# The four slots of the split-weight ring made 32 bytes longer each

## The chip, the cores and the metric

The kernel runs on one core of a Trainium2 chip. The metric is device time in microseconds (us), the median of three runs. Engines are named as in the profile: PE is TensorE's matmul, PEld its weight load, DVE VectorE, ACT ScalarE, POOL GpSimd, SP SyncE, whose queue carries the loads.

## The reference

Two layers of a decoder trunk on 256 tokens of width 1024, in float32. Each layer is a mixer (sliding-window attention, gated short convolution and block attention, all fed by one input projection, each projected back and merged by sigmoid gates, then one output projection), a residual with LayerNorm, and a SwiGLU feed-forward of hidden width 2816 with another residual and LayerNorm:

```python
for l in range(DEPTH):
    mix = hybrid_mixer(x, w_in[l], attn_sinks[l], conv_w[l], w_branch_a[l],
                       w_branch_b[l], w_branch_c[l], w_out[l])
    x = layer_norm(ALPHA * x + mix, ln1_g[l], ln1_b[l])
    ffn = swiglu(x, w_ffn_gate[l], w_ffn_up[l], w_ffn_down[l])
    x = layer_norm(ALPHA * x + ffn, ln2_g[l], ln2_b[l])
```

Nearly all of the arithmetic is products of activations with weights that come once from HBM.

## The kernel before

**Split products.** A float32 product is made of three matmuls in the type float32r: a weight w is split into `wh` (ACT's copy, which rounds, L182) and `wl` = w - `wh` (DVE, L183), an activation likewise into a high and a low part, and wh·high, wh·low and wl·high are added up in PSUM.

**Weight pieces.** All weights lie in HBM as 142 pieces of 128 partitions x 2048 float32 (8192 bytes in each partition). SP loads each into one of three `raw` slots (`load`, from L141); ACT and DVE split it in two halves of 1024 columns (`parts`, L180 to L183) into a tile `wh` and a tile `wl`. Both tags have a ring of `RING = 4` slots in the pool `wts`, so there are eight such tiles. Six pieces of the 142 do not go through the ring: they are split into `wA` and `wB`, in the pool `keep` (the table `place`, L127 to L131).

**What PE does with them.** `mm(acc, a, b)` (L253) issues one matmul: `a` is the stationary operand, loaded by an LDWEIGHTS of 128 columns, and `b` the moving operand, which streams through. The kinds of matmul, by the name of the PSUM tile that they write:

| tile | made by | stationary | moving | columns | matmuls |
|---|---|---|---|---|---|
| acc | `whole` (L357) | wh, then wl | xx | 512, then 256 | 1152 pairs |
| gc | `merge`, `trio` | wh, wh, wl | xx | 256 | 384 |
| br | `branch`, `trio` | wh, wh, wl | y | 256 | 576 |
| hp | `half_pair`, `tokens` | xx | wh, wl, wh | 256 | 576, and 96 with wB |
| cv | `tokens` | xx | wh, wl, wh | 512 | 96 |
| pr, first projection of a layer | `project`, `tokens` | mx | wh, wl, wh | 512 | 144, and 48 with wA |
| pr, second, hidden 0 to 11 | `project` | hidA | wh, wl, wh | 512; 256 | 252; 72 |
| pr, second, hidden 12 to 21 | `project` | hidB | wh, wl, wh | 512; 256 | 168; 48, and 54 with wB |

The rest are 180 transposes (`tp`) and the attention's own products (`s`, `yp`). Of the 1152 pairs of acc, 576 belong to the two feed-forward stages, which run without other matmuls between (272 to 370 and 697 to 795 us of the span); the other 576 belong to the mixers, where `s`, `tp` and `yp` come between.

**What sets the order.** The order on each engine is written out by the class `Plan`, from fixed costs by columns; sizes of tiles do not enter it. The tiles' addresses come from the pools, in the order const, raws, wts, keep, work, each tile rounded up to 32 bytes. In the program as built every ring slot begins at 32 mod 128: `wh` at bytes 44960, 53152, 61344 and 69536 of a partition, `wl` at 77728, 85920, 94112 and 102304. `raw`, `xx`, `mx` and `hidB` begin at 32 mod 128 too; `y`, `hidA`, `wA` and `wB` at 64 mod 128. Each operand of a matmul begins a multiple of 512 bytes behind its tile's start, so it has its tile's residue.

**The start.** Piece 0 is loaded and split in five steps along the inner dimension (L305 to L313: steps of 1, 1, 2, 2 and 2 blocks of 128), each with two ACT copies (L274) and two DVE subtractions (L275), for `xx` and for `wh`, `wl`. PE multiplies each step as it comes.

Of the kernel before, what the change touches and what calls it, by code (L numbers as in the profile page):

```python
# [10 lines left out]
FR = mybir.dt.float32r  # L11
# [5 lines left out]
P = 128  # L17
# [7 lines left out]
PIECE = 2048  # L25
# [22 lines left out]


class Plan:  # L50
    """Orders the instructions of each engine by an estimate (us) of when they can start."""

    HOP = 0.09

# [59 lines left out]
def trunk(ctx: ExitStack, tc: tile.TileContext, x, xt, w, sinks, conv, ln, out):  # L114
# [4 lines left out]
    wts = pool("wts", RING)  # L119
    keep = pool("keep", 1)  # L120
    work = pool("work", 2)
# [1 line left out]
    ctx.enter_context(tc.manual_schedule(engines={ENG.PE, ENG.DVE, ENG.Activation, ENG.SP}))  # L123
    T = Plan()

    # Weight pieces: loaded and split ahead of their use, in the order in which they are used.
    place = {}  # L127
    for l in range(L):
        place[l * PER_LAYER + N_IN + N_BR + N_OUT - 1] = "A"
# [4 lines left out]
    spare, ready, chunks, raw, landed, rawfree = {}, {}, {}, {}, {}, {}  # L134
# [6 lines left out]
    def load(ks=None):  # L141
        j = pos["load"]
        if j >= total:
            return
        pos["load"] += 1
        raw[j] = raws.tile([P, PIECE], FT, name="raw")
        if ks is None:
            for s in cut(j):
                nc.sync.dma_start(raw[j][:, s], w[j][:, s])
        else:  # L150
            a, b = by_k(raw[j]), by_k(w[j])
            for k in ks:
                nc.sync.dma_start(xs[:, k, :], xt[:, k, :])  # L153
                nc.sync.dma_start(a[:, :, k, :], b[:, :, k, :])  # L154
        landed[j] = max(landed.get(j - 1, 2.5), rawfree.get(j - RAWS, 0.0) + 2.0) + 3.0
        open_splits()
# [4 lines left out]
    def open_splits():  # L161
        while pos["split"] < pos["load"]:
            j = pos["split"]
            if j in place:
                if place[j] not in spare:
                    return
                t = spare.pop(place[j])
                both = keep.tile([P, 2, PIECE], FR, tag=place[j], name="w" + place[j])
                ready[j] = both[:, 0, :], both[:, 1, :]
            else:  # L170
                if not slots:
                    return
                t = slots.pop(0)
                ready[j] = wts.tile([P, PIECE], FR, name="wh"), wts.tile([P, PIECE], FR, name="wl")
            pos["split"] += 1
            if j:
                split_piece(j, max(t, landed[j]))
# [7 lines left out]
    def split_piece(j, t, n=CHUNK):  # L185
        def last(task):
            rawfree[j] = task.ready
            load()

        need = T.pe + 5.2 * (j - pos["take"])  # L190
        ss = [slice(c, c + n) for c in range(0, PIECE, n)]
        chunks[j] = [T.add(parts(j, s), t - (1.5 if len(cut(j)) > 1 and not i else 0.0), max(need - t, 0.0) + 0.001 * i, last if s.stop == PIECE else None)
                     for i, s in enumerate(ss)]

    def take():
        j = pos["take"]
        pos["take"] += 1
        T.run()
        T.finish(*chunks.pop(j))
        return j  # L200

    def drop(j):
        if j in place:
            if j % PER_LAYER == N_IN + N_BR + N_OUT:
                spare["B"] = T.pe
        else:
            slots.append(T.pe)
        del ready[j]
        open_splits()

    # Tensor-engine work that waits for a result, issued once the engine has got that far.
    waiting, rounds = [], []
    busy = [0]

# [27 lines left out]
    banks = {"mm": [], "o": []}  # L242

    def bank(shape, tag, name):
        """The next PSUM bank; its last reader four tiles ago is waited for."""
        t = ps.tile(shape, FT, tag=tag, name=name)
        if len(banks[tag]) >= 4:
            for task in banks[tag].pop(0):
                T.finish(task)
        banks[tag].append([])  # L250
        return t, banks[tag][-1]
# [14 lines left out]
    def turn(src, n):  # L266
        tp, users = bank([P, n, P], "o", "tp")
        for i in range(n):
            nc.tensor.transpose(tp[:, i, :], src(i), ident)  # L269
            T.pe += pe_time(2 * P)  # L270
        return tp, users
# [11 lines left out]
    rings = {}  # L283

    def scratch(tag, bufs=2, shape=(P, S)):
        """A work tile for the next task; the task that had its slot before is that task's to wait for."""
        ring = rings.setdefault(tag, [])
        had = ring.pop(0) if len(ring) >= bufs else None
        ring.append(None)
        claims.append((ring, len(ring) - 1, had))  # L290
        return work.tile(list(shape), FT, tag=tag, name=tag, bufs=bufs)
# [60 lines left out]
    def gather(dst, acc):  # L352
        low = scratch("low", 3)
        return copy(low, acc[:, 1, :], S) + [
            dve(S) + (lambda: nc.vector.tensor_add(dst, acc[:, 0, :], low),)]  # L355

    def whole(done, by_step=False):  # L357
        j = take()
        wh, wl = duo(j)
        accs = [bank([P, 2, S], "mm", "acc") for m in range(2)]  # L360
        order = [(m, k) for m in range(2) for k in range(KD)]
        if by_step:
            order.sort(key=lambda mk: mk[1])
        for m, k in order:
            acc, users = accs[m]
            mm(acc, wh[:, m, k, :], xk[k], k == 0, False)
            mm(acc[:, 1, :], wl[:, m, k, :], xk[k][:, 0, :], False, k == KD - 1)
            if k == KD - 1:
                if m:
                    drop(j)  # L370
                done(m, acc, users)
                tick()

    def half_pair(js, h, last):
        acc, users = bank([P, 2, 2, P], "mm", "hp")
        for n in range(2):
            if len(js) == n:
                js.append(take())
            wv = duo(js[n])
            for k in range(KD):  # L380
                tokens(acc[:, n, :, :], [t[:, :, k, :] for t in wv], k, h, xk, k == 0, k == KD - 1)
            if last:
                drop(js[n])
            tick()
        return acc, users

    class Round:
        """A pair of heads: keys and queries split, head a's high part on its own 64 partitions."""

        def __init__(self, when, q, k, new_k, xq, xk, scores):  # L390
            self.when, self.q, self.k, self.new_k, self.xq, self.xk = when, q, k, new_k, xq, xk
# [236 lines left out]
    for l in range(L):  # L628
# [42 lines left out]
        for n in range(2):  # L671
            j = take()
# [16 lines left out]
        for j in range(2):  # L689
# [4 lines left out]
            def conv_h(m, acc, users):  # L694
                hh[m] = scratch("hh")
                made[m] = after(users, gather(hh[m], acc))

            def conv_c(m, acc, users):
                i = 2 * j + m
                t = scratch("t1")  # L700
                u = up[:, i, 2:]
                made[2 + m] = after(users, gather(t, acc) + [("G", 0.69, lambda: nc.gpsimd.tensor_mul(u, t, hh[m]))],
                                    needs=[made[m]])
                z = zs[m] = scratch("t2")

                tap = [cw[:, l, 4 * n + i:4 * n + i + 1].to_broadcast([P, S]) for n in range(3)]
                other = hh[m]

                def taps():
                    nc.gpsimd.tensor_mul(z, up[:, i, 0:S], tap[0])  # L710
                    for n in (1, 2):
                        nc.gpsimd.tensor_mul(other, up[:, i, n:S + n], tap[n])
                        nc.gpsimd.tensor_add(z, z, other)

                made[4 + m] = after([], [("G", 4.0, taps)], needs=[made[2 + m]])
# [87 lines left out]
        merge()  # L803
        spare["A"] = spare["B"] = T.pe
        open_splits()

        hid, last_f = [], {f: [] for f in range(NF)}
# [46 lines left out]
        last = l == L - 1  # L854
# [79 lines left out]
```

## Time and profile before

| | us |
|---|---|
| median of 3 runs (lowest, highest) | 867.87 (866.75, 868.48) |
| span of the profiled execution, first to last instruction | 864.6 |
| median less span | 3.3 |
| PE busy | 852.0 |
| DVE, ACT, POOL busy | 633.3, 485.6, 71.1 |

The profile gives the profiled execution's span and no device time of its own, so sums are made in the span and the 3.3 us are added. A matmul's busy time in the profile reaches past the start of the next one, since matmuls are pipelined: what one costs is read from start to start, or from a stretch of equal ones divided by their number. The chain of work that ended last is listed as stretches with a line and a count, which gives just that. "Idle before" is time in which the engine waited, with what released it.

### The profile page before, as it was taken

What the parts mean: (1) busy time and instruction counts of PE and PEld (TensorE: products, weight loads), DVE (VectorE), ACT (ScalarE), POOL (GpSimd) and SP (SyncE); (2) the same over time, 40 slices, a digit from 0 to 9 for tenths busy, and PEclk for the clock granted to TensorE, in tenths of its full rate; (3) what the DMA queues carried; (4) which work ended last, traced back from release to release, by engine and by line L of the source; (5) the groups of instructions that cost most, each with busy time, mean ns of one, the idle gap of its engine ahead of it and who ended that gap; (6) DMA issues with size and microseconds to landing.
All of it is one profiled execution on the core that took longest, in us unless ns stands there. A gap on an engine that the chain in (4) does not pass through costs nothing.

```text
span 864.6 us, 13385 instructions
## 1 busy us (share of the span) xinstructions
PE 852.0 (99%) x5222; PEld 748.1 (87%) x5222; DVE 633.3 (73%) x1105; ACT 485.6 (56%) x897; POOL 71.1 (8%) x94
## 2 busy tenths in 40 slices
PE   7999999999999999999999999999999999999996
PEld 5978888999899888888898888889998988888885
DVE  5688998766876777755657899986679577777435
ACT  6657677745535666544346767776555265565320
POOL 2003620000100000000000065000000000000000
PEclk9999999999999999999999999999999999999999
DMA  8854444464754555556336343345557365555511
GB/s 295 290 187 155 141 152 146 166 223 163 276 197 159 186 191 195 191 188 227 124 105 242 140 169 124 139 154 196 195 195 249 142 238 177 175 189 196 194 49 49
DMA packets 24815, 155.02 MB, mean 179 GB/s; under 512 B 2704, under 2 KB 4528, under 8 KB 7344
## 3 DMA queue, kind: packets, MB, share of 16 engines
q1 hardware_dynamic: 23536, 149.96, 49.0%
q0 software_dynamic: 1216, 4.22, 1.5%
q8 instruction: 41, 0.67, 0.3%
q14 instruction: 22, 0.18, 0.1%
HBM read 153.11 MB, written 1.05 MB: 178 GB/s over the span
## 4 chain that ended last, share of the span: by engine, by line
PE 97%; DMA 1%; SPq 1%; DVE 1%; ACT 0%; POOLq 0%; issue 0%
PE acc L254 46%; PE pr L254 19%; PE hp L254 9%; PE br L254 8%; PE gc L254 5%; PE s L254 3%; PE cv L254 3%; PE tp L269 2%; PE yp L468 1%; DMA raw<-w 1%; PE yp L470 0%; SPq L154 0%; SPq L153 0%; DVE xtok L496 0%; DVE wl L183 0%; ACT wh L182 0%
## 5 line engine op out<-in xcount | busy, mean ns | idle before, releaser
L254 PE MATMUL acc<-xx,wh 128*128 128x512 f32 x1152 | 411.5, 400 | 5.2 <-ACT wh L274 4.9
L183 DVE TENSOR_TENSOR wl<-raw,wh 128x1024 fp32r<-128x1024 f32 x266 | 325.2, 1243 | 98.5 <-ACT wh L182 97.3
L182 ACT ACTIVATE wh<-raw 128x1024 fp32r<-128x1024 f32 x266 | 272.5, 1052 | 101.8 <-PE pr L254 48.1
L254 PE MATMUL acc<-xx,wl 128*128 128x256 f32 x1152 | 324.8, 282 | 0.2 <-DVE wl L183 0.2
L254 PEld LDWEIGHTS acc<-xx,wh 128*128 128x128 f32 x1152 | 217.6, 189 | 56.7 <-ACT wh L274 6.2
L254 PEld LDWEIGHTS acc<-xx,wl 128*128 128x128 f32 x1152 | 218.9, 190 | 1.5 <-DVE wl L275 0.9
L278 ACT ACTIVATE low<-acc 128x256 f32<-128x256 f32 x144 | 54.2, 380 | 69.7 <-PE acc L254 69.5
L254 PE MATMUL hp<-wh,xx 128*128 128x256 f32 x384 | 72.1, 285 | 0.0
L254 PE MATMUL br<-y,wh 128*128 128x256 f32 x384 | 67.9, 280 | 0.0
L254 PE MATMUL pr<-wh,hidA 128*128 128x512 f32 (+1 forms) x216 | 61.7, 370 | 0.0
L254 PEld LDWEIGHTS hp<-wh,xx 128*128 128x128 f32 x384 | 60.7, 191 | 0.1
L254 PEld LDWEIGHTS br<-y,wh 128*128 128x128 f32 x384 | 59.0, 188 | 0.1
L355 DVE TENSOR_TENSOR t<-acc,low 128x256 f32<-128x256 f32 x88 | 37.0, 420 | 29.9 <-ACT low L278 29.8
L254 PE MATMUL hp<-wl,xx 128*128 128x256 f32 x192 | 54.3, 283 | 0.0
L254 PE MATMUL br<-y,wl 128*128 128x256 f32 x192 | 53.8, 280 | 0.0
L254 PE MATMUL gc<-xx,wh 128*128 128x256 f32 x256 | 46.1, 283 | 0.0
L254 PEld LDWEIGHTS pr<-wh,hidA 128*128 128x128 f32 x216 | 39.0, 188 | 7.7
L254 PE MATMUL pr<-wh,hidB 128*128 128x512 f32 (+1 forms) x144 | 41.9, 367 | 0.0
L499 POOL TENSOR_TENSOR mv<-mv,half 128x1 f32<-128x1 f32 x8 | 7.7, 963 | 398.0 <-DVE mv L490 398.0
L254 PE MATMUL pr<-wl,hidA 128*128 128x512 f32 (+1 forms) x108 | 40.0, 370 | 0.0
L254 PEld LDWEIGHTS gc<-xx,wh 128*128 128x128 f32 x256 | 39.9, 192 | 0.0
L254 PEld LDWEIGHTS hp<-wl,xx 128*128 128x128 f32 x192 | 36.8, 192 | 0.0
(130 smaller groups left out, 1073.1 us busy)
## 6 DMA issues: line engine op xcount, KB each, us to landing
raw<-w SPq DMA_DIRECT2D x136, 1024.0 KB, 4.8
gb<-ln POOLq DMA_DIRECT2D x8, 512.0 KB, 6.1
raw<-w SPq DMA_DIRECT2D x6, 512.0 KB, 6.8
xtok<-x SPq DMA_DIRECT2D x2, 512.0 KB, 6.7
xs<-xt SPq DMA_DIRECT2D x3, 256.0 KB, 4.8
raw<-w SPq DMA_DIRECT2D x3, 256.0 KB, 5.4
out<-xtok SPq DMA_DIRECT2D x3, 256.0 KB, 2.1
xs<-xt SPq DMA_DIRECT2D x2, 128.0 KB, 2.7
```

The lines of the kernel that those rows point to most:

```text
L182: return [act(n) + (lambda: nc.scalar.activation(wh[:, s], raw[j][:, s], AF.Copy),), dve(n) + (lambda: nc.vector.tensor_sub(wl[:, s], raw[ ...
L183: dve(n) + (lambda: nc.vector.tensor_sub(wl[:, s], raw[j][:, s], wh[:, s].bitcast(FT)),)]
L254: nc.tensor.matmul(acc, a, b, start=start, stop=stop)
L269: nc.tensor.transpose(tp[:, i, :], src(i), ident)
L278: return [act(n) + (lambda: nc.scalar.activation(dst, src, AF.Copy),)]
L355: dve(S) + (lambda: nc.vector.tensor_add(dst, acc[:, 0, :], low),)]
L468: nc.tensor.matmul(yp[los[a], :], v[:, 0, vsel[a]], pts[a][:, 0:2, :], start=True, stop=False)
L499: nc.gpsimd.tensor_tensor(mv[:, 3:4], mv[:, 2:3], half, op=OP.pow)
```

## The change

The tiles of the two rings are allocated with 2056 columns and used as their first 2048. A slot takes 8224 bytes of a partition in place of 8192:

```diff
@@ -171,7 +171,7 @@
                 if not slots:
                     return
                 t = slots.pop(0)
-                ready[j] = wts.tile([P, PIECE], FR, name="wh"), wts.tile([P, PIECE], FR, name="wl")
+                ready[j] = [wts.tile([P, PIECE + 8], FR, tag=t_, name=t_)[:, :PIECE] for t_ in ("wh", "wl")]
             pos["split"] += 1
```

The rest of the diff takes out comments and docstrings and keeps the line numbers. In the program as built, the slots then begin at these residues:

| | slot 0 | slot 1 | slot 2 | slot 3 |
|---|---|---|---|---|
| wh, byte of a partition | 44960 | 53184 | 61408 | 69632 |
| wh, mod 128 | 32 | 64 | 96 | 0 |
| wl, byte of a partition | 77856 | 86080 | 94304 | 102528 |
| wl, mod 128 | 32 | 64 | 96 | 0 |

All tiles behind them move up by 8 x 32 = 256 bytes and keep their residue. The two rings do not turn in step: the pieces use, one after the other, the residues (wh, wl) = (32, 32), (0, 0), (96, 64), (64, 96).

No instruction moves on any engine. On ACT, in the five steps of piece 0, the copies of steps 3 and 4 into `wh` wait for DVE besides their DMA (the subtraction that reads the step before):

```order
 L274 ACTIVATE wh<-raw 128x2x256 [waits DMAHW5_49]
 L274 ACTIVATE xx<-xs 128x2x256 [waits DMAHW6_49]
-L274 ACTIVATE wh<-raw 128x2x256 [waits DMAHW7_49]
+L274 ACTIVATE wh<-raw 128x2x256 [waits DMAHW7_49,DVE_49]
 L274 ACTIVATE xx<-xs 128x2x256 [waits DMAHW0_49]
-L274 ACTIVATE wh<-raw 128x2x256 [waits DMAHW1_49]
+L274 ACTIVATE wh<-raw 128x2x256 [waits DMAHW1_49,DVE_49]
```

The two waits are for DVE's sixth and eighth subtraction, the ones into `wl` of steps 2 and 3; each is made by one wait instruction ahead of the copy.

## Rows read from the trace of the kernel before

**Rows 1.** The page's head and engines: busy us, share of the span, instructions.
```profile
span 864.6 us, 13385 instructions
PE 852.0 (99%) x5222; PEld 748.1 (87%) x5222; DVE 633.3 (73%) x1105; ACT 485.6 (56%) x897; POOL 71.1 (8%) x94
PEclk9999999999999999999999999999999999999999
```
**Rows 2.** The page's chain that ended last, shares by engine and line.
```profile
PE 97%; DMA 1%; SPq 1%; DVE 1%; ACT 0%; POOLq 0%; issue 0%
```
**Rows 3.** Who PE waited for: us in total, times, longest.
```profile
PE acc L254 <- ACT wh L274: 4.9, 1, 4.9
PE acc L254 <- DVE xx L275: 0.2, 1, 0.2
PE acc L254 <- DVE wl L183: 0.2, 1, 0.2
```
**Rows 4.** The chain in order of time: start us, us, what, matmuls.
```profile
21.03 8.64 PE hp L254 x72
...
91.55 8.33 PE acc L254 x48
99.88 0.66 PE tp L269 x6
100.53 2.82 PE acc L254 x16
...
164.44 33.92 PE br L254 x288
198.36 23.02 PE gc L254 x192
...
271.86 98.93 PE acc L254 x560
```
**Rows 5.** Timeline of PE, second projection with hidA: start us, us, instruction.
```profile
378.09 0.63 PE L254 MATMUL pr<-wh,hidA 128*128 128x512 f32 x2
...
379.49 0.40 PE L254 MATMUL pr<-wh,hidA 128*128 128x512 f32 x1
```
**Rows 6.** Timeline of PE, second projection with hidB.
```profile
407.85 0.39 PE L254 MATMUL pr<-wl,hidB 128*128 128x512 f32 x1
...
409.21 0.39 PE L254 MATMUL pr<-wl,hidB 128*128 128x512 f32 x1
```
**Rows 7.** Timeline of PE, first projection, from piece wA to a ring piece.
```profile
230.84 1.56 PE L254 MATMUL pr<-wA,mx 128*128 128x512 f32 x6
232.24 0.39 PE L254 MATMUL pr<-wh,mx 128*128 128x512 f32 x1
...
233.40 0.62 PE L254 MATMUL pr<-wh,mx 128*128 128x512 f32 x2
...
234.08 0.62 PE L254 MATMUL pr<-wh,mx 128*128 128x512 f32 x2
```
**Rows 8.** Lines L182 and L183: duration ns min/median/max, first and last start.
```profile
L182 ACT ACTIVATE wh<-raw x266: 1037/1051/1071, 13.0 to 830.8; 128x1024 fp32r<-128x1024 f32 x133
L182 ACT ACTIVATE wB<-raw x8: 1046/1051/1066, 223.9 to 828.9; 128x1024 fp32r<-128x1024 f32 x8
L183 DVE TENSOR_TENSOR wl<-raw,wh x266: 1209/1220/1761, 14.1 to 832.4; 128x1024 fp32r<-128x1024 f32 x133
L183 DVE TENSOR_TENSOR wB<-raw,wB x8: 1215/1218/1226, 225.4 to 830.1; 128x1024 fp32r<-128x1024 f32 x8
```
**Rows 9.** Timeline of the start: ACT, DVE and PE in steps 2 to 4.
```profile
8.42 0.69 DVE L275 TENSOR_TENSOR wl<-raw,wh 128x512 fp32r<-128x512 f32 x1
...
10.36 0.63 ACT L274 ACTIVATE wh<-raw 128x512 fp32r<-128x512 f32 x1 [0.55 <-DMA raw<-w]
...
11.02 0.69 DVE L275 TENSOR_TENSOR wl<-raw,wh 128x512 fp32r<-128x512 f32 x1 [0.49 <-ACT wh L274]
...
11.72 0.63 ACT L274 ACTIVATE wh<-raw 128x512 fp32r<-128x512 f32 x1
...
12.97 1.06 ACT L182 ACTIVATE wh<-raw 128x1024 fp32r<-128x1024 f32 x1 [0.62 <-DMA raw<-w]
...
13.35 0.40 PE L254 MATMUL acc<-xx,wh 128*128 128x512 f32 x1
...
13.58 0.28 PE L254 MATMUL acc<-xx,wl 128*128 128x256 f32 x1
```

## The prediction

> **What bounds the kernel now.** I read the page's engines first: PE is busy 852.0 of 864.6 us, and its clock stands in the top tenth, the 2.4 GHz level, in every slice [rows 1]. The chain that ended last agrees: 97% of it is PE [rows 2]. Then who PE waited for: 5.3 us in three waits, all at the start [rows 3]. So behind the start nothing that ACT, DVE or the loads do ends last, and the change can act in one way alone: if PE's own matmuls go faster or slower because their weights begin elsewhere. What a matmul costs I take from stretches of the chain, each divided by its count [rows 4], and, for 512 columns, from PE's timeline, start to start.
>
> Pure streaming at 2.4 GHz would be 106.7 ns for 256 columns and 213.3 for 512. No kind reaches that, and the surplus differs with the starts of the two operands:
>
> - Weights and partner both at 32 mod 64: hp 8.64/72 = 120.0 ns, gc 23.02/192 = 119.9 [rows 4]; 512 columns with hidB, six matmuls from 407.85 to 409.21, 226.7 ns [rows 6].
> - One at 32 and the other at 64: br 33.92/288 = 117.8 ns [rows 4]; 512 columns with hidA, six from 378.09 to 379.49, 233.3 ns [rows 5]. With wA moving and mx stationary it is 233.3 as well: six from 230.84 to 232.24 [rows 7].
> - After such a stretch the equal kind doesn't find its pace at once: from 232.24 to 233.40 five matmuls take 232.0 ns each, and only then, from 233.40 to 234.08, three take 226.7 [rows 7].
> - The pairs of acc have equal starts throughout and yet two paces: 2 x 8.33/48 = 347.1 ns in the mixer, and behind the next transposes 2 x 2.82/16 = 352.5; 2 x 98.93/560 = 353.3 through a whole feed-forward stage [rows 4]. So the starts are not all: the pace into which PE falls also hangs on what ran just before, and it can keep the worse one for 99 us.
>
> Only two residues occur before, 32 and 64 mod 128; the change brings 0 and 96 as well. I reckon with mod 64: 96 as 32 and 0 as 64. No row shows that; it is my choice, since it needs no pace that the trace lacks.
>
> **The change part by part.** Counted in the program as built, by each matmul's own weight slice:
>
> 1. 256 columns. 288 of hp and 192 of gc go from equal to different: 480 x (117.8 - 120.0) = -1.1 us. 272 of br become equal: 272 x 2.2 = +0.6. Together -0.5 us. The 120 of 256 columns in the last projection I set at nothing; at 2.2 ns they are worth 0.3 us at most.
> 2. 512 columns. 40 of cv, 80 with mx and 84 with hidB go from equal to different: 204 x 6.6 = +1.3 us. Of those with hidA 134 become equal. But half of all pieces have wh and wl of different kind (96 with 64), so that equal and different alternate after one or two matmuls, and five are needed to find the pace [rows 7]. So of the 134 half get 226.7 (67 x 6.6 = -0.4) and half 232 (67 x 1.3 = -0.1), and of the 204 that stay equal with mx, hidB and cv half rise from 226.7 to 232: 102 x 5.3 = +0.5. Together +1.3 us.
> 3. acc, nearly half of the chain. No row has a pair with different starts. The nearest are 512 and 256 columns apart, 233.3 + 117.8 = 351.1 ns, and I take that. It lies between the two paces of now. In the feed-forward 288 of 576 pairs change: 288 x (351.1 - 353.3) = -0.6 us. In the mixers 288 change; by the chain some 320 of the 576 run at 346.7 to 347.1 and the rest at about 353, so 160 x 4.4 = +0.7 and 128 x -2.2 = -0.3. Of the 288 feed-forward pairs that stay equal, each piece now comes behind one of another kind, as those of the mixer come behind other work, and may fall into the better pace; I take one in four: 72 x -6.6 = -0.5. Together -0.7 us. The bounds are wide. Every pair at the best pace of the rows: 832 pairs (576 of the feed-forward, 256 of the mixers) x -6.4 = -5.3 us. Above, no row has a steady pace over 353.3; if the better pace were lost everywhere, 320 x 6.4 = +2.0, and if every one of the 576 changed pairs lost a further 7 ns, the step from one kind to the other that 512 columns show, +4.0: together +6.0.
> 4. ACT's writes and DVE's reads and writes of the slots. Ring halves at 32 take 1051 and 1220 ns (median), halves of wB, at 64, take 1051 and 1218 [rows 8]. Nothing; and were a half some tens of ns slower, ACT and DVE have slack (56% and 73% busy, and PE waits for neither behind the start).
> 5. The two new waits. Step 3's copy starts at 10.36, held by its DMA; the subtraction it now waits for began at 8.42 and took 0.69, so it is done at 9.11. Step 4's copy starts at 11.72; its new wait ends with the subtraction that runs from 11.02 to 11.71 [rows 9]. It slips by the passing of the semaphore and the wait instruction, by my estimate under 0.1 us (DVE follows ACT's copy of 10.36 to 10.99 at 11.02, 0.03 us). Behind it on ACT stands the next piece's copy, which waits for its DMA until 12.97 anyway; DVE's subtraction of step 4 would slip with it and end near 13.2 in place of 13.1. PE first wants this step's wh at 13.35 and its wl at 13.58 [rows 9]. Cost nothing; without that cover, 0.1 us.
> 6. Loads, the other tiles and their order: the raw slots stay where they are, tiles behind move by 256 bytes and keep their residue. Nothing.
>
> Sum: -0.5 + 1.3 - 0.7 = +0.1 us on a span of 864.6. With the 3.3 us around it: 868.0.
>
> A word on a rule that speaks against any such effect. The Trainium skill (SBUF — State Buffer, Specifications) has SBUF read in lines of 16 bytes. All starts, before and after, are multiples of 32, so by it every slice covers the same lines and each term above is nothing: the span would stay at 864.6. The rows agree with it for ACT and DVE and disagree for PE, where 117.8 stands against 120.0 and 233.3 against 226.7 with no other difference of columns; I hold to the rows.
>
> **The rivals.**
>
> *The good paces need all slots alike (slower).* 226.7 and 347 were only seen in runs of equal starts. If any change of residue between neighbours breaks them, and the unlike kind's gain for 256 columns doesn't come (br has other operands than gc, so its 117.8 may belong to y and not to the difference), then cv, mx and hidB pay 408 x 6 = +2.4 us, the mixers' 320 pairs +2.0, br 576 x 2.2 = +1.3: +5.7, 873.6. It starts to decide when more than a third of that arrives without the gains of term 1. For it: the relocking in rows 7. Against: gc and hp show nothing to break.
>
> *The change shakes the feed-forward out of its worse pace (faster).* PE keeps 353.3 for two whole stages because nothing disturbs it; in the mixers, behind other work, it falls into 347 for 48 matmuls at a time. With residues turning every 5.7 us, all pieces may settle at the better pace or below: -5.3 from term 3, with term 1's -0.5 and half of term 2: about -5, 863. For it: acc is nearly half of the chain. Against: half of the pieces mix their kinds and have no row at all.
>
> *The starts don't matter to PE, or the old ones are simply replaced by equals (no change).* Then 867.9, within the forecast's own range.
>
> *The new residues 0 and 96 have paces of their own.* No row speaks for or against; it widens the range to both sides.
>
> **How the numbers follow.** No change 0.38, slower 0.27, faster 0.35. A measurement of this kernel can tell about 0.2%, 1.7 us, from no change; my sum lies well inside, but its terms are of that size and each pace of acc is a guess between the rows, so the sides together get more than half; the faster side more than the slower, since more of the work runs at a bad pace now than at a good one (832 pairs against 320). The no-change case alone ranges over 866.3 to 869.7. The range for 8 in 10 goes from the faster rival's 863 less 1 to the slower rival's 873.6: 862 to 873.5.
>
> **What would show it.** PE's timeline: start to start of gc and hp pieces, 120.0 or 117.8 by the piece's residue; of hidB near 233 and of hidA a mixture; the feed-forward stage's length, 98.9 us now. It is right if that stage stays within 98 to 100 and the other stretches move by under 1 us each; wrong if one residue gives a pace that no row of before has, such as pairs well under 347 or over 354, or if PE waits for ACT or DVE behind the first 15 us.

## The result and the profile after

The changed kernel takes 862.36 us (862.00 to 862.64, five runs), before 867.87: ratio 0.9933, 95% interval 0.9913 to 0.9953. It is 5.5 us faster, outside the range that I gave for no change and near the figure of the faster rival (863). The spans of the two profiled executions differ by 4.0 us (864.6 and 860.6); the medians stand 3.3 and 1.8 us above them. In every execution whose span was taken, device time less its own span is 1.7 to 1.9 us, so the 3.3 us that the forecast added hold some 1.5 us by which the profiled execution of before was faster than the median one. The rows below explain the 4.0.

PE of the changed kernel still does 96% of the chain, and waits 5.6 us, 5.3 before [rows 2, 3]. Who PE waited for (us in total, times, longest):

```profile
PE acc L254 <- ACT wh L274: 5.4, 3, 4.5
PE tp L269 <- DVE xtok L496: 0.2, 1, 0.2
```

So the time came out of PE's own matmuls. The chain in order of time (start us, us, what, matmuls), to be laid beside [rows 4]:

```profile
21.23 8.51 PE hp L254 x72
...
91.51 8.37 PE acc L254 x48
...
100.53 2.79 PE acc L254 x16
...
164.49 33.89 PE br L254 x288
198.37 22.72 PE gc L254 x192
...
271.83 97.33 PE acc L254 x560
369.16 57.00 PE pr L254 x246
...
694.54 97.28 PE acc L254 x560
```

The two feed-forward stages fall from 98.93 us to 97.33 and 97.28: 347.5 ns a pair in place of 353.3, together -3.25 us. gc falls by 0.3 us a layer, hp from 120.0 to 118.2 ns a matmul, which is -1.0 us over its 576. br stays (33.92 and 33.89); the mixers' acc, added up start to start over both traces, falls by 0.4 us. The second projection of layer 0 took 56.85 us for its 246 matmuls and takes 57.00.

Within a stage the pace turns with the pieces. Two neighbouring pieces on PE's timeline (start us, us, instruction), the first with wh and wl at 32 mod 128, the second with both at 0:

```profile
299.51 0.39 PE L254 MATMUL acc<-xx,wh 128*128 128x512 f32 x1
...
300.55 0.39 PE L254 MATMUL acc<-xx,wh 128*128 128x512 f32 x1
...
303.32 0.40 PE L254 MATMUL acc<-xx,wh 128*128 128x512 f32 x1
...
304.37 0.39 PE L254 MATMUL acc<-xx,wh 128*128 128x512 f32 x1
```

Three pairs from 299.51 to 300.55 are 346.7 ns each, three from 303.32 to 304.37 are 350. The first piece has the residues of before mod 128 and yet the better pace, which before was seen only in the mixers. Mod 256 it does not have them: the four longer slots of wh push the whole ring of wl up by 128 bytes, so wl begins at 32 mod 256, where before it began at 160 like wh and xx.

### The profile page after: what moved, and what is told of

Read it like the earlier page. It is cut to its first block, busy times and chain, and to the rows that moved or that the text cites. A ratio compares the mean times of both kernels' runs of the same rounds, so it can differ in the third digit from the quotient of the medians.

```text
span 860.6 us, 13387 instructions
## 1 busy us (share of the span) xinstructions
PE 847.7 (99%) x5222; PEld 746.6 (87%) x5222; DVE 633.9 (74%) x1105; ACT 486.8 (57%) x897; POOL 71.3 (8%) x94
## 4 chain that ended last, share of the span: by engine, by line
PE 96%; DMA 2%; DVE 1%; SPq 0%; issue 0%; ACT 0%; POOLq 0%; POOL 0%; DVEq 0%
PE acc L254 47%; PE pr L254 18%; PE hp L254 9%; PE br L254 8%; PE gc L254 5%; PE s L254 3%; PE cv L254 3%; PE tp L269 2%; PE yp L468 1%; DMA gb<-ln 1%; DMA raw<-w 1%; PE yp L470 0%; DVE xtok L496 0%; SPq L153 0%; DVE wA L183 0%
## 5 line engine op out<-in xcount | busy, mean ns | idle before, releaser
L183 DVE TENSOR_TENSOR wl<-raw,wh 128x1024 fp32r<-128x1024 f32 x266 | 325.4, 1244 | 97.2 <-ACT wh L182 96.0
L182 ACT ACTIVATE wh<-raw 128x1024 fp32r<-128x1024 f32 x266 | 273.0, 1054 | 101.1 <-PE pr L254 49.0
L254 PEld LDWEIGHTS br<-y,wl 128*128 128x128 f32 x192 | 36.2, 188 | 0.0
```

Of the source, the lines that this page charges most:

```text
L182: return [act(n) + (lambda: nc.scalar.activation(wh[:, s], raw[j][:, s], AF.Copy),), dve(n) + (lambda: nc.vector.tensor_sub(wl[:, s], raw[ ...
L183: dve(n) + (lambda: nc.vector.tensor_sub(wl[:, s], raw[j][:, s], wh[:, s].bitcast(FT)),)]
L254: nc.tensor.matmul(acc, a, b, start=start, stop=stop)
```

## The experiments

Distances are counted in bytes from xx (160 mod 256), or for br from y (192), to wh and wl, mod 256; before, all pieces are at (0, 0) from xx, and in the changed kernel none is. Theory A says that it takes residues which turn from piece to piece, B and C that each distance has a pace of its own (B counts mod 128, C mod 256), H that PE holds one of several steady paces at the same starts, chosen by what ran before.

**Uniform residues: u32, u64, u96, u0.** Slots of 8320 bytes, 65 x 128, used from column `o` = 0, 8, 16 or 24:

```diff
-                ready[j] = wts.tile([P, PIECE], FR, name="wh"), wts.tile([P, PIECE], FR, name="wl")
+                ready[j] = [wts.tile([P, PIECE + 32], FR, tag=t_, name=t_)[:, o:o + PIECE] for t_ in ("wh", "wl")]
```

Expected of u32: 

> All eight ring slots 8320 bytes long and used from their first byte, so that every weight begins at 32 mod 128 as before, but neighbours differ by 128 mod 256; the two added ACT waits are not there. Theory A (turning: the residues that alternate from piece to piece throw PE out of the 353.3 ns cycle; equal residues leave it in whatever cycle it entered): 867.9, feed-forward stage 98.9 us. Theory B (own pace: each distance between the two operands' starts has a pace of its own, whatever ran before): the changed kernel's pieces with 32 and 32 ran at 346.9 ns a pair, so 864 to 865 and a feed-forward stage of 97.1 us. If the length of the slot or 256 mattered, neither.

Expected of u64: 

> All weights of the ring at 64 mod 128, nothing turning. Theory A: no gain from turning; pairs of acc keep one pace through the stage, by the rows for unlike starts 350 to 351, feed-forward 98.0 to 98.3 us, whole kernel 866 to 868. Theory B: the pair's pace depends on the distance of weights from xx (32 bytes here); the changed kernel's pieces at 0 (distance -32) ran at 350, so again 350 and 98.0; br (y at 64, distance 0) 120.0, gc and hp 117.8: 866 to 867. Theories differ little here; what counts is whether 64 and 0 cost the same.

Expected of u96: 

> All weights of the ring at 96 mod 128, 64 bytes from xx, mx and hidB. Theory A with residues counted mod 64: as at 32, 867.9 and a feed-forward stage of 98.9 us, gc and hp at 120.0. Theory B with residues counted mod 128: in the changed kernel br at distance 64 (wh and wl at 0, y at 64) ran at 113.5 ns a matmul, and the pieces (96, 64) at 346.8 a pair, so gc and hp 113.5 (960 x -6.5 = -6 us) and acc 346.8 or less (-3.8 us or more): 858 or less.

Expected of u0: 

> All weights of the ring at 0 mod 128. Theory A: one pace for the stage, that of the changed kernel's pieces at 0: 350 ns a pair, feed-forward 98.0 us. Theory B: the same 350 for acc, but br at distance 64 from y runs at 113.5 in every piece (576 x -4.3 = -2.5 us): 863 to 865. Under A with residues mod 64, br at 120.0: 867 to 869.

Measured, as ratio to before with its interval: u32 864.76 us, 0.9971 (0.9960 to 0.9982); u64 866.34, 0.9988 (0.9979 to 0.9997); u96 865.34, 0.9977 (0.9967 to 0.9986); u0 860.42, 0.9923 (0.9909 to 0.9936). u64's time and stage fit A and B alike. The other three met no theory as a whole: u32's time fits B, but its stage of 98.20 us fits neither; u96 gained in gc and not in acc; u0 is faster than any forecast for it. Their chains: u32's first feed-forward stage;

```profile
272.49 98.20 PE acc L254 x560
```

u96's gc and stage;

```profile
200.57 21.97 PE gc L254 x192
272.89 98.49 PE acc L254 x560
```

u0's stage and the br of both its layers.

```profile
164.15 33.33 PE br L254 x288
...
270.68 97.43 PE acc L254 x560
...
586.48 32.68 PE br L254 x288
```

gc at 64 bytes from xx takes 114.4 ns a matmul in u96, averaged over its four pieces (119.9 before), br at 64 bytes from y 113.5 in u0's second layer and 115.7 in its first (117.8 before). These are paces that no row of before had. Slots of 65 x 128 bytes turn by 128 mod 256, and that shows: in the first stage of each kernel, worked out start to start over whole pieces without the first few and the last, a pair of acc takes (ns)

| kernel | (wh, wl) distance and pace |
|---|---|
| before | (0, 0) 353.3 |
| after | (0, 128) 346.9; (96, 224) 349.6; (64, 160) 346.8; (32, 192) 346.7 |
| u32 | (0, 0) 353.2; (128, 128) 350.5; (0, 128) 346.9; (128, 0) 351.4 |
| u64 | (32, 32) 353.5; (160, 160) 350.1; (32, 160) 350.2; (160, 32) 349.7 |
| u96 | (64, 64) 353.3; (192, 192) 353.3; (192, 64) 347.0; (64, 192) 353.5 |
| u0 | (96, 96) 346.7; (224, 224) 347.3; (224, 96) 348.0; (96, 224) 350.1 |

Pieces alike mod 128 but not mod 256 differ (u32), so my count mod 64 was wrong, and mod 128 would have been too. And turning is not enough for the better pace: u32's pieces at (0, 0) come behind unlike ones each time and still run at 353.2, and three of u96's four kinds at 353.3 and 353.5.

**One distance for all pieces: d0_128, d192_64.** Slots of 8192 bytes, nothing turns. wl has a pool of its own and is pushed up by gaps (a gap is a pool with one small tile that GpSimd zeroes once); in d192_64 the slots of y, hidA, wA and wB move to 160 mod 256 as well. Not shown are the helper `gap`, the line that takes wl from `wlo`, and the 56 columns added to the tile `mix` in d192_64:

```diff
+    gap("gap0", 0)        # d192_64: 192
     wts = pool("wts", RING)
+    gap("gap1", 128)
+    wlo = pool("wlo", RING)
+    gap("gap2", 128)      # d192_64: 192
```

Expected of d0_128: 

> Slots of 8192 bytes as before, nothing turning; the ring of wl alone is moved up by 128 bytes, so wh begins at 160 and wl at 32 mod 256 (xx at 160). Theory C (the pace of a kind follows from the distances of wh and wl from the other operand, each mod 256): all pieces are the changed kernel's (32, 32) pieces, 346.9 ns a pair: feed-forward stage 97.1 to 97.4 us (98.9 before), gc 22.9 (23.0 before; 0.8 ns a matmul less), hp 118 to 118.5, cv and pr of mx and hidB slower by 2 to 3 ns of 228; in all 864 to 865. Theory A (the gain comes from residues that turn): 98.9 and 867.5. With residues counted mod 128 only: 867.5 too.

Expected of d192_64: 

> Nothing turns; wh at 96 and wl at 224 mod 256, distances 192 and 64 from xx, mx and hidB at 160, and the tiles of the slot of y, hidA and wA moved to 160 as well (wB follows to 160). Theory C, from the pieces at (192, 64) in the runs before: acc 346.8 ns a pair in the mixers and the feed-forward (97.1 us a stage), gc 113.4 a matmul (21.8 us), br 113.4 (32.7 us), hp 117.8, pr with mx and hidB some 229, with hidA 228.5: -3.7 -1.6 -2.5 -2.5 -1.2 and -0.5 us, 855 to 857. Theory A: no turning, so the feed-forward stage may stay at 98.9; with the gains of br and gc (-5.0), 861 to 863.

Measured: d0_128 864.56 us, 0.9973 (0.9960 to 0.9986); d192_64 862.71, 0.9950 (0.9938 to 0.9963). Both stages run at the better pace throughout; d0_128:

```profile
277.74 97.08 PE acc L262 x560
...
700.46 97.07 PE acc L262 x560
```

So it takes no turning: A falls. The stages are 0.2 us shorter than the changed kernel's. In the profiled execution of d0_128 (868.13 us) PE waits 4.0 us behind the start, so its stretches are read here and not its span. But in d192_64 br stands at (192, 64) from y, where three of u0's pieces ran at 113.4 and a fourth at 118.8, and doesn't take the faster pace. Nor does gc, at (192, 64) from xx:

```profile
164.83 34.24 PE br L262 x288
199.07 22.82 PE gc L262 x192
...
272.30 97.07 PE acc L262 x560
```

That is 118.9 ns a matmul for both. C promised 32.7 us for br and 21.8 for gc; over two layers the two miss that by 5.1 us, most of the whole miss (862.7 against 855 to 857). So C falls as well.

One might think that the places themselves count, and not the distances. u0 shows that they don't settle it either. The first and the fifth piece of br in layer 0 lie in the same two slots, wh at 128 and wl at 0 mod 256 (y at 192):

```profile
165.06 0.40 PE L254 MATMUL br<-y,wh 128*128 128x256 f32 x2
...
166.84 0.40 PE L254 MATMUL br<-y,wh 128*128 128x256 f32 x2
...
187.11 0.39 PE L254 MATMUL br<-y,wh 128*128 128x256 f32 x2
...
189.15 0.39 PE L254 MATMUL br<-y,wh 128*128 128x256 f32 x2
```

From 165.06 to 166.84 fifteen matmuls take 118.7 ns each, from 187.11 to 189.15 eighteen take 113.3.

**All starts as before, PE disturbed: shake, shake1.** One extra matmul into an unused PSUM tile, ten times (shake) or twice (shake1; the comments give its values):

```diff
         for f in range(4, NF):
+            if f % 4 == 0:                                  # shake1: f == 6
+                n = (64, 32, 96, 16, 48)[f // 4 - 1] + 64 * l   # shake1: (96, 160)[l]
+                dm, _ = bank([P, S], "o", "dm")
+                mm(dm[:, :n], xx[:, 0, 0, 0:P], xx[:, 0, 0, :n], True, True)
```

Expected of shake: 

> The kernel before, all starts unchanged; in each feed-forward stage one extra matmul of xx by xx into an unused PSUM tile, of 64, 32, 96, 16 or 48 columns (64 more in layer 1), ahead of the pieces 4, 8, 12, 16 and 20, so ten disturbances in all, each some 0.05 to 0.15 us (1 us together). Theory H (at equal starts PE holds two paces, 346.7 and 353.3 a pair, and what ran just before chooses): behind some of the ten the pace changes to 346.7 and stays until the next; if half do, the two stages win 1.9 us in all and the kernel is at 867 or below. Theory C alone (the distances fix the pace): every stretch stays at 353.3 and the kernel is slower by 1 us, 868.5.

Expected of shake1: 

> All starts as in the kernel before; one extra matmul in each feed-forward stage, of 96 columns in layer 0 and 160 in layer 1, ahead of the third of its 18 whole pieces. Theory H: if it hits the same point of the three-pair cycle as in the run with ten, pairs run at 346.7 from there on: 16 pieces x 16 pairs x 6.6 ns = 1.7 us less a stage, 97.3 us and 864.2 in all, most of what the change won in these stages (3.3 us), with no start changed. If starts alone decide: 98.9 and 867.6.

Measured: shake 866.36 us, 0.9987 (0.9976 to 0.9998); shake1 865.27, 0.9980 (0.9964 to 0.9996). PE's timeline of shake around the third disturbance of layer 0, of 96 columns:

```profile
314.01 0.40 PE L254 MATMUL acc<-xx,wh 128*128 128x512 f32 x1
...
315.07 0.40 PE L254 MATMUL acc<-xx,wh 128*128 128x512 f32 x1
...
315.42 0.21 PE L254 MATMUL dm<-xx 128*128 128x96 f32 x1
...
316.23 0.39 PE L254 MATMUL acc<-xx,wh 128*128 128x512 f32 x1
...
317.27 0.39 PE L254 MATMUL acc<-xx,wh 128*128 128x512 f32 x1
```

Three pairs ahead of it take 1.06 us (353.3 each), three behind it 1.04 (346.7), and the better pace lasts for the rest of the stage, through two further disturbances. The two ahead of it (64 and 32 columns) changed nothing. Start to start, the worse pace is a cycle of three unequal pairs (241 + 120, 236 + 113, 232 + 118 ns); in the better one all are alike (230 + 117). In layer 1 the third disturbance, of 160 columns, hit in the same way, and the fifth, of 112, put PE back:

```profile
783.53 0.39 PE L254 MATMUL acc<-xx,wh 128*128 128x512 f32 x1
...
784.57 0.40 PE L254 MATMUL acc<-xx,wh 128*128 128x512 f32 x1
...
784.91 0.21 PE L254 MATMUL dm<-xx 128*128 128x112 f32 x1
...
786.09 0.40 PE L254 MATMUL acc<-xx,wh 128*128 128x512 f32 x1
...
787.15 0.40 PE L254 MATMUL acc<-xx,wh 128*128 128x512 f32 x1
```

Three pairs take 1.04 us ahead of it and 1.06 behind. The other seven of shake's ten changed nothing, one of 96 columns in layer 1 among them, so the width alone does not decide.

In shake1 the one of layer 1 hit and that of layer 0 missed; its chain, for the 512 matmuls behind each:

```profile
280.92 90.51 PE acc L254 x512
...
705.98 88.78 PE acc L254 x512
```

353.6 ns a pair and 346.8. So at equal starts PE has two steady paces in the same code, and one matmul of some 0.1 us moves it from one to the other. That is H, shown for the pairs of acc; whether the extra matmul acts by its time or by its mere place between the others is not told apart. I expected 864.2 for two hits; with one hit 865.3 is in line.

**One half of the change: padwl.** Only the wl slots are longer. That moves more than wl: all tiles behind the ring go up by 128 bytes, so xx lies at 32 mod 256 and wh 128 bytes from it.

```diff
-                ready[j] = wts.tile([P, PIECE], FR, name="wh"), wts.tile([P, PIECE], FR, name="wl")
+                ready[j] = wts.tile([P, PIECE], FR, name="wh"), wts.tile([P, PIECE + 8], FR, name="wl")[:, :PIECE]
```

Expected of padwl: 

> One half of the change: only the wl slots are 32 bytes longer and turn through 32, 64, 96, 0 mod 128; wh stays at one residue (128 mod 256 from xx). Theory A and H (turning, or any unlike neighbour, keeps PE out of the 353.3 cycle): feed-forward stages 97.1 to 98.2 us and 862 to 865. If both rings must turn: 98.9 and 867.5.

Measured: 863.01 us, 0.9944 (0.9924 to 0.9965), the stage 97.71 us:

```profile
272.20 97.71 PE acc L254 x560
```

Half of the edit gives most of the gain, as expected; it doesn't need both rings. It doesn't tell turning from new starts, since no piece of padwl is at (0, 0) either.

**Towards the best: d224_96, d96_96.** As d0_128, with gaps of 224, 128 and 160 bytes, and of 96, 0 and 160.

Expected of d224_96: 

> Nothing turns: wh at 128 and wl at 0 mod 256, so 224 and 96 from xx, mx and hidB, 192 and 64 from y and hidA, which stay where they are. If PE takes the better pace at these starts as it did in the pieces that had them: feed-forward stages 97.1 to 97.8 us (98.9 before), br 113.4 a matmul in most pieces (32.8 us a layer, 33.9 before), hp 117, mx and hidB 233: 858 to 860, below the changed kernel and u0. If the pace is a matter of what ran before (theory H), br may as well stay at 118 without the turning, as it did in d192_64: 861 to 863.

Expected of d96_96: 

> Nothing turns: wh and wl both at 0 mod 256, 96 from xx, mx and hidB and 64 from y and hidA. By the pieces of u0 with these distances: feed-forward 97.1 us, br 113.4 or 117.8 a matmul, hidA 227.5, hp 120, mx, hidB and cv 231 to 233: 858 to 861 with the fast br, 861 to 863 without. Theory H allows either.

Measured: d224_96 858.84 us, 0.9904 (0.9879 to 0.9930); d96_96 861.53, 0.9930 (0.9904 to 0.9956). d224_96 has the lowest median of all, 8.6 us under before as measured beside it (867.45) and 3.5 under the changed kernel, whose interval its own overlaps. The chain shows where from:

```profile
164.59 32.67 PE br L262 x288
...
270.33 97.08 PE acc L262 x560
...
585.52 32.67 PE br L262 x288
```

br runs at 113.4 ns in all pieces (33.89 us a layer in the changed kernel), the feed-forward at the better pace. d96_96 has the same two stretches and is a little slower than its forecast of 858 to 861; its hp gains nothing (119.9 ns a matmul, worked out start to start, 117.2 in d224_96).

## Why the prediction was wrong

- *What bounds the kernel.* Right: PE alone, and the change acted through the pace of its matmuls, but for 0.2 us that a transpose waited for DVE. ACT and DVE halves kept their times (1053 and 1221 ns, median; 1051 and 1220 before). The Trainium skill's lines of 16 bytes (SBUF — State Buffer, Specifications), by which no start here should matter, don't tell of PE's paces. The measurement decides: br took 113.4 ns a matmul in d224_96 and 118.9 in d192_64.
- *Step 1, 256 columns, -0.5 us.* Right in sign, too small: gc -0.6 and hp -1.0 us, br 0.0 in place of +0.6, about -1.6. The added cost of br's equal pieces didn't come, since some of its pieces, at 64 bytes from y, run faster than any row of before (114.5).
- *Step 2, 512 columns, +1.3 us.* Right as a sum: added up start to start over both traces, cv +0.2, pr with mx +0.8, with hidB +0.6 and with hidA -0.4, together +1.2. The good pace of 226.7 with hidB [rows 6] was lost and hidA's bad one [rows 5] bettered, as worked out. But the sorting of pieces behind it does not hold: hidB's pieces with both residues of before mod 128 were to keep 226.7 and run at 232.6. That the sum fits is in part luck.
- *Step 3, acc, -0.7 us.* This is the step that failed: it measured -3.6. The two feed-forward stages won 3.25 us where I had 1.1, and the mixers' pairs won 0.4 where I had them lose 0.4. I took 351.1 ns for the changed pairs; the crossed ones (96 with 64) run at 346.7 to 346.8, and only those at 0 near it, at 349.6. Of the "unchanged" feed-forward pairs I let one in four fall into the better pace; behind the first pieces all run at 346.9 to 347.0. They weren't unchanged: mod 256 their wl stands 128 bytes from xx, and d0_128, with that one distance in every piece and nothing turning, holds 346.7 through both stages. So 353.3 was one of two paces that PE has at (0, 0), as shake shows; the changed kernel has no piece there.
- *The faster rival.* Its 863 us, to which I gave 0.35, is met, its reason is not borne out. I had turning shake PE out of 353.3; but d0_128 gains without turning, and u32's pieces at (0, 0) turn and stay at 353.2. That its figure fits is luck in part.
- *What would show it.* By its own signs the prediction is wrong: the stage left 98 to 100 us (97.3), and some pieces of br have a pace that no row of before has.
- *My count mod 64.* Wrong: u32's pieces differ by 128 mod 256 and run at different paces, and u96's gc and u0's br at 64 bytes take paces that 0 did not.
- *The two waits of step 5.* Right. Step 4's copy idles 0.18 us for DVE, more than the 0.1 I allowed, and nobody waits for it:

```profile
11.98 0.63 ACT L274 ACTIVATE wh<-raw 128x512 fp32r<-128x512 f32 x1 [0.18 <-DVE wl L275]
```

The first hp stretch starts 0.2 us later than before (21.23 against 21.03), but the first matmul began 0.4 earlier. I did not test that part by itself; in shake, with the start of before, that stretch begins at 21.59, so 0.2 us is within what single executions differ by.

What stays open is why PE has such paces at all. The runs show which starts and which disturbances led where, not the mechanism. That d192_64's br stays at 118.9, that d224_96's takes 113.4 from its first piece on, and that u0's changes from 118.7 to 113.3 in the same slots, is seen and not explained. Nor was a second pace looked for at the other distances, so 346.7 need not be the only one there.

## What to carry to other kernels

Where one engine is busy 99% of the span, read its pace start to start by stretch: equal work at two paces (347 and 353 ns a pair here) can be time to be won without moving an instruction. Where the operands begin in SBUF is worth trying in steps of 32 bytes up to 256, measured and not reasoned; half a line of code gave 5.5 us of 868, the best placing 8.6. And a kernel that only differs in an address or in one tiny matmul can differ by 0.2 to 1%, so such a difference is no verdict on what else a change does.

## What the hardware showed that I had not expected

- The same pairs at the same addresses run at 353.3 or 346.7 ns, and one extra matmul of 96 columns switched it for the rest of a stage; one of 112 switched it back (shake).
- 256-column matmuls take from 113.3 to some 120 ns by where their two operands begin and by what ran before; the same slots gave 118.7 and 113.3 (u0). Pieces alike mod 128 but not mod 256 differ (u32).
- ACT's and DVE's passes over the weights took 1051 and 1220 ns a half before [rows 8] and 1053 and 1221 (medians) over the changed kernel's four residues.
